# A hybrid layer on one core: tokens also passed transposed, k and v of tile one computed by token, and small VectorE steps woven into other work

## The chip, the core and the metric

The kernel runs on one core of a Trainium2 chip. The metric is the device time of one execution in microseconds (us), as the median over the runs shown. A profile of one execution comes with it: for each engine the instructions with their times, waits and the source lines that issued them. The engines are TensorE (PE in the profile, its weight loads PEld), VectorE (DVE), ScalarE (ACT), GpSimd (POOL) and SyncE (SP, which here only issues DMA transfers).

## What is computed

One decoder layer on 2048 tokens of 1024 channels, in float32. A normed input feeds one projection whose columns are split into nine parts; a short convolution branch and a sliding-window attention branch follow; their projections are merged by gates and added to the input.

```python
h = rms_norm(x, norm_g)                       # x: 1 x 2048 x 1024
u = h @ w_in                                  # conv v, B, C, z | q, k, v, z_a | gates
y_c = b_c * causal_depthwise_conv(c_c * v_c, conv_w) * silu(z_c)
y_a = y_c @ w_conv_out
q = rms_norm(q, q_norm_g); k = rms_norm(k, k_norm_g)     # 16 q heads, 4 k/v heads of 64
o = sliding_window_attention(q, k, v, sinks) * silu(z_a) # window 128, a sink per head
y_b = o @ w_attn_out
g_a, g_b = split(sigmoid(gate_logits + gate_b))
out = x + (g_a * y_a + g_b * y_b) @ w_out
```

`rms_norm` divides each token (each head of a token, for q and k) by the root of its mean square and multiplies by a gain per channel. So `h = x * g * r`, with a root `r` for each token; and since `r` is one number for a token, `h @ w = r * ((x * g) @ w)`.

## The kernel before

**Precision.** Float32 products are made from pairs: each operand is split into a high part (rounded to the matmul's input type, a cast on ScalarE) and a low part (what the cast left out, a subtraction on VectorE), and each product is three matmuls, high x high, high x low, low x high (lines 362 to 371).

**Tiles and units.** Tokens are taken in two tiles of 1024, each in two halves of 512 (`H`), each half in four blocks of 128. Channels come in eight chunks of 128 (`KC`). The activations are kept with channels on partitions and tokens along the free axis, so that a matmul has a 128x128 block of weights as its stationary operand and 512 tokens as the moving one. Most of the work is done in units `sunit` (line 379): a 256-column by 1024-token piece of a projection in seven products instead of eight, in the manner of Strassen. A unit's products run in the order 1, 5, 6, 2, 7, 3, 4, twelve matmuls each. The weights of a unit are prepared by `pieces_of` (264): two loads, high and low parts, and four 128x1024 additions or subtractions (`sums`, 292) for the operands that are sums. The token operands of the seven products are sums and differences of the two halves and of neighbouring chunks; they are kept in `ops`, and made by `form` (545, one split of a chunk held in `raw`) or `direct` (500, a split straight out of PSUM). In tile one, k and v are the exception: `cunit` (409) makes them by channel with the four plain blocks, eight products of 12 matmuls for each, so only operands 1, 2, 8 and 3 are needed for them.

**Order.** The schedule is manual: each engine executes its instructions in the order in which the code issues them. `run` (line 555) drives a unit; each step of twelve matmuls is a tick. After a tick's matmuls it issues the weight loads that have room, the high part of a prepared weight piece (ScalarE), whatever was put down for that tick with `put(n, f)` (551), and then the low part of the weight piece (VectorE). `mids` holds work issued in the middle of a product of `cunit`. So the place of every small step is a number written by hand. SP issues the loads of weights and of attention's operands; POOL issues the stores of q, k and v to DRAM and the token loads of tile two.

**The start** (lines 1107 to 1214). SP loads four token tiles of 128 x 1024 (`x_load`), the first weight half, four more token tiles, and the next weight halves. ScalarE sums the squares (`x_square`); VectorE makes the roots in a chain of some eleven small dependent steps (`x_rsqrt`, `rsqrt` at 191), and the tokens are scaled (`x_scales`). TensorE transposes each chunk of a half with four 128x128 transposes (`x_turn`, 480), and the operands come out of PSUM with the gain applied (`direct`, `x_raw`, `less`). The gains, the convolution taps, the biases and the sinks are loaded as rows by ScalarE's and POOL's queues and transposed on TensorE (`prep_gain`, `prep_cols`). Before all of it TensorE runs 23 and then 14 clearing matmuls on a tile of zeros (`WARM`, `WARM2`, lines 1131 to 1138). Then come k and v of the first half, k and v of the second, and the four q units; the operands of the second half and the sums are put between them.

**After the projection of q.** The conv units, gates and z units follow, with attention steps (`att_load` to `att_out`) put between them, then `ya` and `yb`, the two branch projections (line 970). While `yb` of tile one runs, `next_tile` (1235) prepares tile two: POOL loads the tokens, ScalarE squares them, VectorE makes roots and scales, and `turn_l`/`turn_r` transpose the 64 blocks and make the operands. Tile two then goes the same way, with k and v as units `sunit`. `out` (`fin_o`) ends the kernel.

**q, k and v.** A q result goes through `fin_q` (595): copied from PSUM, split, stored to DRAM by POOL's queue, transposed in groups of four (`turn4`), squared and reduced per head, its roots made at a later tick. `fin_k` (637) transposes k, norms it, transposes it back (`back`) and stores its parts; `fin_v` (682) transposes v and stores it. Attention loads all of it back.

Of the kernel before, what the change touches and what calls it, by code (L numbers as in the profile page):

```python
# [31 lines left out]
WARM = 24  # L32
WARM2 = 14
# [10 lines left out]
def block_kernel(  # L44
# [3 lines left out]
    norm_g: bass.AP,  # L48
    w_in: bass.AP,
    conv_w: bass.AP,  # L50
    q_norm_g: bass.AP,
    k_norm_g: bass.AP,
    sinks: bass.AP,
    w_conv_out: bass.AP,
    w_attn_out: bass.AP,
    gate_b: bass.AP,
# [6 lines left out]
    x2, out2, w_in2 = x[0], out[0], w_in[0]  # L63
# [48 lines left out]

    ident = consts.tile([P, P], F32, name="ident")
# [10 lines left out]
    for h in range(2):  # L124
        nc.vector.tensor_copy(mask_i[HALVES[h]], mask_f[HALVES[h], h, :])
    negc = consts.tile([P, HD], F32, name="negc")
    nc.gpsimd.memset(negc, NEG)
    zero = slot([P, H], F32R, "zero")
    zf = zero.bitcast(F32)
    nc.gpsimd.memset(zf, 0.0)  # L130

    sink_bc = consts.tile([P, NH], F32, name="sink_bc")

    sink_r = consts.tile([P, NKV, 2, 2], F32, name="sink_r")
    nsink_r = consts.tile([P, NKV, 2, 2], F32, name="nsink_r")


    R_B, R_Q = 3 * KC, 5 * KC
    NR = 5 * KC + 2
    rows_g = slot([KC, P], F32, "rows_g")  # L140
    nc.scalar.dma_start(rows_g, norm_g.rearrange("o (c p) -> (o c) p", p=P))
    cols_g = consts.tile([P, KC], F32, name="cols_g")
    rows = slot([NR, P], F32, "rows")

    def load_rows(xt):

        seen = small.tile([P, 1], F32, tag="sx", bufs=4, name="seen")
        nc.gpsimd.tensor_copy(seen, xt[:, 0:1])
        nc.gpsimd.dma_start(sink_bc, sinks.partition_broadcast(P))
        nc.gpsimd.dma_start(rows[0:R_B, :], conv_w.rearrange("t (c p) -> (t c) p", p=P))  # L150
        nc.gpsimd.dma_start(rows[R_B:R_Q, :], gate_b.rearrange("o (c p) -> (o c) p", p=P))
        for i, gsrc in enumerate((q_norm_g, k_norm_g)):
            for j in range(2):
                nc.gpsimd.dma_start(rows[R_Q + i : R_Q + i + 1, j * HD : (j + 1) * HD], gsrc)

    cols = consts.tile([P, NR], F32, name="cols")
# [8 lines left out]
    def prep_gain():  # L165
        pt0 = mbank("ptg")
        nc.tensor.transpose(pt0[:, 0, :KC], rows_g, ident[:KC, :KC])
        nc.vector.tensor_copy(cols_g, pt0[:, 0, :KC])

    def prep_cols():  # L170
        pt0 = mbank("pt0")
        nc.tensor.transpose(pt0[:, 0, :NR], rows, ident[:NR, :NR])
        nc.vector.tensor_copy(cols, pt0[:, 0, :NR])
        nc.vector.tensor_scalar(
            out=gqk, in0=cols[:, R_Q : R_Q + 1], scalar1=cols[:, R_Q + 1 : R_Q + 2],
            scalar2=HD ** -0.5, op0=ALU.mult, op1=ALU.mult)
        nc.vector.tensor_scalar(
            out=hbias, in0=cols[:, R_B:R_Q], scalar1=0.5, scalar2=None, op0=ALU.mult)
        sv = sink_bc.rearrange("p (j c e) -> p j c e", c=2, e=2)
        for e in range(2):  # L180
            for h in range(2):
                nc.vector.tensor_copy(sink_r[HALVES[e], :, h, :], sv[HALVES[e], :, :, e])
        nc.vector.tensor_scalar(out=nsink_r, in0=sink_r, scalar1=-1.0, scalar2=None, op0=ALU.mult)
# [7 lines left out]
    def rsqrt(a, n, name):  # L191
# [3 lines left out]
        nc.vector.tensor_scalar(  # L195
            out=t.bitcast(I32), in0=a.bitcast(I32), scalar1=1, scalar2=None,
            op0=ALU.logical_shift_right)
        nc.vector.tensor_scalar(
            out=r.bitcast(I32), in0=t.bitcast(I32), scalar1=-1, scalar2=RSQRT_MAGIC,
            op0=ALU.mult, op1=ALU.add)  # L200
        for _ in range(3):
            nc.vector.tensor_tensor(out=t, in0=r, in1=r, op=ALU.mult)
            nc.vector.scalar_tensor_tensor(
                out=t, in0=t, scalar=-0.5, in1=a, op0=ALU.mult, op1=ALU.mult)
            nc.vector.scalar_tensor_tensor(
                out=r, in0=t, scalar=1.5, in1=r, op0=ALU.add, op1=ALU.mult)
        return r

    def split(hi, lo, src):
        nc.scalar.copy(hi, src)  # L210
        return nc.vector.tensor_tensor(out=lo, in0=src, in1=hi.bitcast(F32), op=ALU.subtract)  # L211

    def add(o, a, b, eng=None):
        return (eng or nc.vector).tensor_tensor(out=o, in0=a, in1=b, op=ALU.add)  # L214

    def sub(o, a, b, eng=None):
        return (eng or nc.vector).tensor_tensor(out=o, in0=a, in1=b, op=ALU.subtract)

    def mul(o, a, b, eng=None):
        return (eng or nc.vector).tensor_tensor(out=o, in0=a, in1=b, op=ALU.mult)  # L220
# [6 lines left out]
    def load_half(i=None, first=None):  # L227
# [8 lines left out]
        if kind in "SC":  # L236
            raw = rawpool.tile([P, 2, KP, P], F32, tag="raw", name=name)
            if first:
                first(raw)
# [24 lines left out]
    def pieces_of(n):  # L264
# [7 lines left out]
        def two(hi, lo, src):  # L272
            return (lambda: nc.scalar.copy(hi, src),
                    lambda: nc.vector.tensor_tensor(
                        out=lo, in0=src, in1=hi.bitcast(F32), op=ALU.subtract))

        if kind in "SC":
# [11 lines left out]
            if kind == "C":  # L289
                return w, [(2, 1, lambda h=h: pair(h, (h, 0), (h, 1), f"c{h}")) for h in range(2)]  # L290

            def sums():
                ra, rb = raws[2 * n], raws[2 * n + 1]

                def f():
                    sub(ra[:, 0], ra[:, 0], rb[:, 0])
                    add(rb[:, 0], rb[:, 0], rb[:, 1])
                    sub(rb[:, 1], rb[:, 1], ra[:, 0])
                    sub(ra[:, 1], ra[:, 1], rb[:, 1])

                return (lambda: None, f)

            return w, [(2, 0, lambda: pair(0, 1, 2, "a")), (1, 0, single), (0, 0, sums),
                       (2, 1, lambda: pair(1, 5, 6, "s")), (2, 1, lambda: pair(0, 7, 3, "t"))]
# [17 lines left out]
    def piece():  # L322
# [4 lines left out]
        need = [2 * n + i] if plan[n][0] in "TC" else [2 * n, 2 * n + 1][: 1 + min(i, 1)]  # L327
# [32 lines left out]
    mids = {}  # L360
# [18 lines left out]
    def sunit(key, ops, fin):  # L379
# [7 lines left out]
        yield  # L387
        vb = bank(f"V{nm}")
# [7 lines left out]
        product(xb, u, 2, ops, False)  # L396
        fin(0, 0, xb)
        yield
# [10 lines left out]
    def cunit(key, ops, fin, q, hold):  # L409

        if q == 0:
            hold[key] = unit(key)
        u = hold[key]
        for i in range(2):
            ps = bank(f"C{key[0]}_{i}_{q}")
            for p in range(2):
                force(u, (i, p))
                hi, lo = ready[u][i, p]
                for j in range(KP):
                    b = ops[B_AT[p, q]][j]  # L420
                    for n, (w, m) in enumerate(((hi, 0), (hi, 1), (lo, 0))):
                        nc.tensor.matmul(
                            ps, lhsT=w[:, j, :], rhs=b[:, m, :], start=p == 0 and j == 0 and n == 0,
                            stop=p == 1 and j == KP - 1 and n == 2)
                    if j == 1:
                        for f in mids.pop(tick[0], []):
                            f()
                if p == 0:
                    yield
            fin(i, q, ps)  # L430
            live[0] -= 2 * q
            yield

    def into(dst, val):
        if isinstance(val, tuple):
            add(dst, *val)
        else:
            nc.scalar.copy(dst, val)
# [9 lines left out]

    def x_load(t, b, eng):
# [5 lines left out]
    def x_square(xt, junk, ss, i):  # L455

        nc.scalar.activation(out=junk, in_=xt, func=AF.Square, accum_out=ss[:, i : i + 1])

    def x_rsqrt(t, b0, n, ss):
        ms = small.tile([P, n], F32, tag="sm", name=f"ms{t}_{b0}")  # L460
        nc.vector.tensor_scalar(out=ms, in0=ss, scalar1=1.0 / D, scalar2=EPS, op0=ALU.mult, op1=ALU.add)
        return rsqrt(ms, n, f"hr{t}_{b0}")

    def x_scale(xt, r, i, act, cs=slice(0, D)):
        if act:
            nc.scalar.activation(out=xt[:, cs], in_=xt[:, cs], func=AF.Copy, scale=r[:, i : i + 1])
        else:
            nc.vector.tensor_scalar(
                out=xt[:, cs], in0=xt[:, cs], scalar1=r[:, i : i + 1], scalar2=None, op0=ALU.mult)

    def x_scales(xs, q, r):
        for i in range(HB):
            xt = xs[q * HB + i]
            if i < 3:
                x_scale(xt, r, i, i == 2)
            else:
                x_scale(xt, r, i, False, hs(0))
                x_scale(xt, r, i, True, hs(1))

    def x_turn(t, q, c, xs, pt=None):  # L480
        if pt is None:
            pt = mbank(f"pth{t}_{q}_{c}")
        for b in range(HB):
            nc.tensor.transpose(pt[:, b, :], xs[q * HB + b][:, c * P : (c + 1) * P], ident)
# [888 lines left out]
```

## Time and profile before

| what | us |
|---|---|
| median of three runs | 2014.37 (2012.85 to 2015.1) |
| the profiled execution | 2012.82 |
| its span, first to last instruction | 2011.1 |

Where TensorE stands in that span, from the busy time by stretch (PE busy, VectorE busy):

| stretch, us | length | PE | DVE | what runs |
|---|---|---|---|---|
| 0 to 13.59 | 13.59 | 10.96 | 4.82 | loads, squares, roots; clearing matmuls |
| 13.59 to 98.55 | 84.96 | 80.48 | 71.21 | k and v of tile one, the first q unit |
| 98.55 to 162.09 | 63.54 | 63.27 | 50.64 | the three other q units |
| 162.09 to 861.00 | 698.91 | 695.04 | 480.53 | conv, gates, z, attention, ya |
| 861.00 to 948.33 | 87.33 | 87.33 | 60.65 | yb; tile two prepared |
| 948.33 to 2011.10 | 1062.8 | 1055.1 | 715.6 | tile two and out |

The last row is two stretches added. A busy share is read with care: the clearing matmuls of the first 13.59 us are busy time too, and they compute nothing of the result. The granted TensorE clock is 1.00 in all rows, which is the hardware's full rate.

### The profile page before, as it was taken

The numbers are of one execution on the slowest core, as the hardware profiler recorded it, in microseconds if no ns is written. First come the engines' busy times: TensorE is split into PE (matmuls) and PEld (weight loads), VectorE is DVE, ScalarE is ACT, GpSimd is POOL, SyncE is SP. The second block draws the span as 40 slices with busy tenths as digits, with TensorE's granted clock in tenths as the row PEclk, the third lists the DMA queues.
The fourth block names the chain that finished last, engine by engine and source line by source line (L and its number), as shares of the span: only waits on it lengthen the run. The fifth ranks groups of instructions, "written<-read, shape, count | busy, mean of one in ns | idle before, by whom it ended". The sixth has DMA issues, their size and how long they took to land.

```text
span 2011.1 us, 27717 instructions
## 1 busy us (share of the span) xinstructions
PE 1992.2 (99%) x9360; PEld 1656.5 (82%) x9360; DVE 1383.4 (69%) x2361; ACT 934.0 (46%) x1847; POOL 375.3 (19%) x521
## 2 busy tenths in 40 slices
PE   8999999999999999999999999999999999999999
PEld 6788888888888888888888888888888888888887
DVE  6878878787775565358777887887776656356654
ACT  7554454456664343244555454556665334212321
POOL 1462222123330000000263212212322000100000
PEclk9999999999999999999999999999999999999999
DMA  5485444457564535764486434555665434865553
GB/s 170 126 216 129 130 122 131 121 164 203 163 184 159 182 105 173 231 208 155 113 211 173 120 109 134 142 142 176 184 187 185 151 122 147 259 210 168 169 173 110
DMA packets 336317, 324.61 MB, mean 161 GB/s; under 512 B 25788, under 2 KB 256240, under 8 KB 336176
## 3 DMA queue, kind: packets, MB, share of 16 engines
q1 hardware_dynamic: 323136, 284.78, 47.1%
q0 software_dynamic: 13024, 38.06, 7.3%
q8 instruction: 75, 1.23, 0.3%
q14 instruction: 66, 0.54, 0.1%
q10 hardware_dynamic: 16, 0.00, 0.0%
HBM read 226.00 MB, written 96.73 MB: 160 GB/s over the span
## 4 chain that ended last, share of the span: by engine, by line
PE 90%; DVE 4%; ACT 3%; issue 2%; DMA 1%; POOL 0%; SPq 0%; POOLq 0%; ACTq 0%; DVEq 0%
PE Y L368 28%; PE yb L970 9%; PE ya L970 8%; PE Xcv L368 4%; PE Vcv L368 4%; PE Vb L368 2%; PE Xb L368 2%; PE Xza L368 2%; PE Vz L368 2%; PE Vo L368 2%; PE Xz L368 2%; PE Xo L368 2%; PE Vza L368 2%; PE po L840 2%; PE Vq L368 2%; PE Xq L368 2%
## 5 line engine op out<-in xcount | busy, mean ns | idle before, releaser
L823 POOL TENSOR_SCALAR_AFFINE_SELECT xh<-xh 64x512 fp32r<-64x512 f32 x64 | 67.6, 1056 | 654.8 <-DVE xl L815 524.3
L794 ACT ACTIVATE p<-s,st,rq 128x128 f32<-128x128 f32 x256 | 113.3, 453 | 0.5
L214 DVE TENSOR_TENSOR o<-po,o 64x256 f32<-64x256 f32 x128 | 53.7, 419 | 58.6 <-ACT o L851 56.2
L1004 DVE SCALAR_TENSOR_TENSOR tha<-tha,ya 128x512 f32<-128x512 f32 x32 | 22.0, 688 | 92.4 <-PE ya L970 90.7
L851 ACT COPY o<-po 64x256 f32<-64x256 f32 x128 | 47.0, 367 | 82.4 <-DVE o L214 80.9
L815 DVE TENSOR_TENSOR xl<-pt,xh 128x512 fp32r<-128x512 f32 x64 | 44.2, 691 | 56.0 <-ACT yp L814 49.0
L970 PE MATMUL ya<-opa,wya_1h 128*128 128x512 f32 x256 | 79.6, 391 | 0.9 <-ACT opa L210 0.5
L368 PE MATMUL Xcv<-oph,wcv_ah 128*128 128x512 f32 x256 | 79.8, 393 | 0.0
L970 PE MATMUL yb<-opb,wyb_0h 128*128 128x512 f32 x256 | 79.5, 392 | 0.0
L970 PE MATMUL yb<-opb,wyb_1h 128*128 128x512 f32 x256 | 79.5, 392 | 0.0
L970 PE MATMUL ya<-opa,wya_0h 128*128 128x512 f32 x256 | 78.9, 389 | 0.0
L210 ACT CAST opb<-ocr 128x512 fp32r<-128x512 f32 x32 | 19.9, 621 | 112.2 <-DMA ocr<-ocd 107.2
L1024 DVE SCALAR_TENSOR_TENSOR thb<-thb,yb 128x512 f32<-128x512 f32 x32 | 22.0, 686 | 55.2 <-PE yb L970 55.2
L970 PEld LDWEIGHTS ya<-opa,wya_1h 128*128 128x128 f32 x256 | 48.1, 188 | 12.2 <-ACT opa L210 1.3
L698 POOL DMA_DIRECT2D vd<-v x32 | 20.2, 637 | 200.6 <-DVE v L211 197.6
L970 PEld LDWEIGHTS ya<-opa,wya_0h 128*128 128x128 f32 x256 | 48.1, 188 | 10.0
L970 PEld LDWEIGHTS yb<-opb,wyb_1h 128*128 128x128 f32 x256 | 47.6, 188 | 9.6
L970 PEld LDWEIGHTS yb<-opb,wyb_0h 128*128 128x128 f32 x256 | 47.6, 188 | 9.6
L368 PEld LDWEIGHTS Xcv<-oph,wcv_ah 128*128 128x128 f32 x256 | 47.0, 188 | 9.0
L823 POOL TENSOR_SCALAR_AFFINE_SELECT yp<-xl 64x512 fp32r<-64x512 f32 x64 | 53.6, 838 | 3.1
L889 DVE SCALAR_TENSOR_TENSOR y<-u,cols,y 128x512 f32<-128x512 f32 x64 | 49.1, 767 | 6.2 <-ACT y L882 5.0
L813 ACT CAST xh<-pt 128x512 fp32r<-128x512 f32 x64 | 37.4, 585 | 33.4 <-PE pt L810 32.2
(586 smaller groups left out, 6281.5 us busy)
## 6 DMA issues: line engine op xcount, KB each, us to landing
wcv_raw<-in_w_in SPq DMA_DIRECT2D x64, 256.0 KB, 3.7
q<-q2d SPq DMA_DIRECT2D x64, 256.0 KB, 4.1
v<-vd SPq DMA_DIRECT2D x128, 128.0 KB, 3.3
gd<-th SPq DMA_DIRECT2D x64, 256.0 KB, 2.3
wq_raw<-in_w_in SPq DMA_DIRECT2D x32, 256.0 KB, 4.5
q2d<-q_h POOLq DMA_DIRECT2D x64, 128.0 KB, 3.8
q2d<-q_l POOLq DMA_DIRECT2D x64, 128.0 KB, 4.1
kq<-q2d SPq DMA_DIRECT2D x128, 64.0 KB, 4.0
```

The costliest lines, as they stand in the source:

```text
L214: return (eng or nc.vector).tensor_tensor(out=o, in0=a, in1=b, op=ALU.add)
L368: nc.tensor.matmul(ps, lhsT=w[:, j, :], rhs=b[:, m, :], start=start and j == 0 and i == 0, stop=j == KP - 1 and i == 2, skip_group_check=n ...
L794: nc.scalar.activation(out=p[:, i, :], in_=sg[:, i, HD : 3 * HD], func=AF.Exp, bias=st[:, 1, i : i + 1], scale=rv[:, i // 2, i % 2 : i % 2 ...
L813: nc.scalar.copy(xh, pt)
L815: nc.vector.tensor_tensor(out=xl, in0=pt, in1=xh.bitcast(F32), op=ALU.subtract)
L823: nc.gpsimd.affine_select(out=d4, in_=s4, pattern=[[0, 2 * G], [-sg, HD]], compare_op=ALU.is_gt if prev else ALU.is_ge, fill=0.0, base=0, ...
L840: nc.tensor.matmul(po[:, cs], lhsT=v2[:, kind, :], rhs=xx.rearrange("p g q -> p (g q)")[:, cs], start=n == 0, stop=n == 2)
L851: nc.scalar.copy(ov, pov[oth, :, :, e, :])
L889: nc.vector.scalar_tensor_tensor(out=y, in0=u[:, h * H + i : h * H + i + H], scalar=tap(i, k), in1=y, op0=ALU.mult, op1=ALU.add)
L970: nc.tensor.matmul(ps, lhsT=w[:, j, cs], rhs=o[:, m, :], start=n == 0 and i == 0, stop=n == KC - 1 and i == 2)
L1004: nc.vector.scalar_tensor_tensor(out=m, in0=m, scalar=1.0, in1=ps, op0=ALU.add, op1=ALU.mult)
L1024: nc.vector.scalar_tensor_tensor(out=m, in0=m, scalar=1.0, in1=ps, op0=ALU.add, op1=ALU.mult)
```

## The change

The inputs now also hold `xt`, the tokens transposed (1024 channels by 2048 tokens), and `consts`, one array with taps, biases, q and k gains, gains and sinks already laid out by partition; both are laid out by the host without arithmetic (`_layout`).

*Tile one, loads.* SP alternates chunk halves of `xt` (128x512, 256 KB) with w pieces of a new kind "R": 128 rows by 512 columns, k and v side by side. The natural token tiles are still loaded, behind them, but only for the sums of squares.

```diff
+    FIRST_X = {(0, 0): (1,), (0, 1): (2, 3), (1, 0): (4,), (1, 1): (5,), (2, 0): (6,), (2, 1): (7,)}
...
+    xt_load(0, 0)
+    for n in range(3):
+        load_half(n)
+    xs[0] = x_load(0, 0, nc.sync)
+    load_half(3)
+    for b in range(1, HB):
         xs[b] = x_load(0, b, nc.sync)
+    for c in range(KC):
+        xt_load(c, 1)
     for b in range(HB, NB):
         xs[b] = x_load(0, b, nc.sync)
...
-    for _ in range(WARM - 1):
-        clear()
-    prep_gain()
-    for _ in range(WARM2):
-        clear()
+    for _ in range(WARM):
+        nc.tensor.matmul(Y, lhsT=zero[:, :P], rhs=zero, start=True, stop=True)
```

`WARM` is 10 (24 and 14 before), and the zeros are written by VectorE instead of POOL. The eight loads of constants as rows and the two transposes of them go, with the copies of sinks into place.

*Tile one, k and v by token, from unscaled tokens.* `plain_op` splits a chunk with the gain but without the root. In `kv_by_token` the tokens are stationary (128 of them) and 512 columns of k and v move, so a result has tokens on partitions: eight banks, the same 192 matmuls. The root of a token is then a number for a partition, and is applied when the result leaves PSUM, in the class `KV`, which takes the place of `cunit`, `fin_k` and `fin_v` in tile one.

```diff
+    def plain_op(c, q):
+        o = new_op("p", B_AT[c % 2, q], c // 2, plain_ops)
+        h = raw[c, q]
+        nc.scalar.activation(out=o[:, 0], in_=h, func=AF.Copy, scale=gain(c))
+        vec.scalar_tensor_tensor(
+            out=o[:, 1], in0=h, scalar=gain(c), in1=o[:, 0].bitcast(F32),
+            op0=ALU.mult, op1=ALU.subtract)
...
+                for k, (m, w) in enumerate(((0, hi), (0, lo), (1, hi))):
+                    nc.tensor.matmul(
+                        ps, lhsT=x[:, m, i * P : (i + 1) * P], rhs=w[:, c % 2],
+                        start=c == 0 and k == 0, stop=c == KC - 1 and k == 2)
...
+            for b in (2 * n, 2 * n + 1):
+                v = slot([P, NKV, 2, HD], F32R, f"v0_{b}")
+                src = self.banks[b][:, UC:].rearrange("p (j d) -> p j d", d=HD)
+                r = rtok[:, b : b + 1]
+                nc.scalar.activation(out=v[:, :, 0], in_=src, func=AF.Copy, scale=r)
+                vec.scalar_tensor_tensor(
+                    out=v[:, :, 1], in0=src, scalar=r, in1=v[:, :, 0].bitcast(F32),
+                    op0=ALU.mult, op1=ALU.subtract)
```

The first eight ticks make the four blocks of the first half, chunk by chunk as the loads land (two score banks and two others); two groups of four ticks make the second half. k is still transposed back (`back`), v no longer is transposed.

*Turned roots.* For q and all that follows, the tokens must be scaled where tokens lie along the free axis. `x_roots` broadcasts each column of 128 roots and transposes it, so every partition gets the roots as a row; `x_norm` multiplies a chunk half by gain and row in one step. It replaces scaling and transposing the tokens in both tiles; the sums for the operands, which `less` made out of PSUM, become plain subtractions (`first_sum`, `second_sum`, `third`, `t4`).

```diff
+    def x_roots(t, q, rs):
+        pt = mbank(f"ptr{t}_{q}")
         for b in range(HB):
+            nc.tensor.transpose(pt[:, b, :], rs[:, b : b + 1].to_broadcast([P, P]), ident)
+        rb = slot([P, H], F32, f"rb{t}_{q}")
+        nc.scalar.copy(rb, pt.rearrange("p b q -> p (b q)"))
+        return rb
...
+    def x_norm(h, c, rb):
+        vec.scalar_tensor_tensor(
+            out=h, in0=h, scalar=gain(c), in1=rb, op0=ALU.mult, op1=ALU.mult)
...
+    put(3, lambda: roots(0))
+    put(6, lambda: turned(0))
...
+    put(6, lambda: norm_l(0, 2, st))
...
+    put(8, lambda: form(0, 1, 1, st))
```

The places of these steps over ticks 1 to 21 are again written by hand (some 80 `put` lines, of which four are shown).

*Woven steps.* All VectorE operations of the kernel now go through `vec`, which issues one waiting step of a chain behind each operation; the chains are the roots (`rsqrt`) and three of the four weight sums. Five more are issued at each tick's end (`WOVEN`), and whoever needs a chain's result issues what is left of it.

```diff
+        def some(self, n):
+            for _ in range(n):
+                self.one()
+        def __getattr__(self, name):
+            f = getattr(nc.vector, name)
+            def g(*args, **kw):
+                r = f(*args, **kw)
+                self.one()
+                return r
+            return g
```

*Tile two.* `next_tile` loads `xt` of tile two chunk by chunk (`raw_load`, 16 loads on POOL's queue), beside the natural tokens for the squares; two groups of four transposes make the root rows, and `norm_l`, `norm_r` and the sums take the place of `turn_l` and `turn_r`.

*Smaller.* The split of q of the first unit is put three ticks later (`QWAIT`); the casts of a mask go from VectorE to POOL. `sunit` gets an order in which product 2 comes second; with `Q_TWO = 0` it isn't used.

By count, TensorE loses 144 transposes (160 go, 16 come) and 28 clearing matmuls, VectorE gains 42 two-tensor steps of 512 and loses 8 scalings and 3 steps of 1024, ScalarE loses 23 steps of 512 and 6 of 1024 and gains 12 copies, POOL gains 16 loads and loses 7, SP gains 24 loads of 256 KB.

More of the change, by code (lines that the diff above doesn't have):

```diff
@@ L110, in hs @@
         return slice(q * H, (q + 1) * H)
+    cols = consts.tile([P, NC], F32, name="cols")
+    nc.scalar.dma_start(cols, consts_in)
+    zero = slot([P, H], F32R, "zero")
+    zf = zero.bitcast(F32)
+    nc.vector.memset(zf, 0.0)
+    seen = small.tile([P, 1], F32, tag="sx", bufs=4, name="seen")
+    nc.scalar.activation(out=seen, in_=zf[:, 0:1], func=AF.Square)
     ident = consts.tile([P, P], F32, name="ident")
@@ L124, in block_kernel @@
     for h in range(2):
-        nc.vector.tensor_copy(mask_i[HALVES[h]], mask_f[HALVES[h], h, :])
+        nc.gpsimd.tensor_copy(mask_i[HALVES[h]], mask_f[HALVES[h], h, :])
     negc = consts.tile([P, HD], F32, name="negc")
     nc.gpsimd.memset(negc, NEG)
[L128 to L134, printed above, removed]
-    nsink_r = consts.tile([P, NKV, 2, 2], F32, name="nsink_r")
[L138 to L156, printed above, removed]
+    sink_r = cols[:, C_S:NC].rearrange("p (j h c) -> p j h c", h=2, c=2)
+    nsink_r = consts.tile([P, NKV, 2, 2], F32, name="nsink_r")
     gqk = consts.tile([P, 1], F32, name="gqk")
@@ L387, in sunit @@
         yield
+        if two:
+            product(xb, u, 2, ops, False)
+            fin(0, 0, xb)
+            yield
         vb = bank(f"V{nm}")
@@ L395, in sunit @@
         yield
-        product(xb, u, 2, ops, False)
-        fin(0, 0, xb)
-        yield
+        if not two:
+            product(xb, u, 2, ops, False)
+            fin(0, 0, xb)
+            yield
         product(Y, u, 7, ops, False)
```

632 lines of the change are left out of this document (366 added, 266 removed).

## The prediction

> **What bounds the kernel now.** I read the page first: busy shares and the chain of work that ended last.
>
> ```profile
> PE 1992.2 (99%) x9360; PEld 1656.5 (82%) x9360; DVE 1383.4 (69%) x2361; ACT 934.0 (46%) x1847; POOL 375.3 (19%) x521
> ...
> PE 90%; DVE 4%; ACT 3%; issue 2%; DMA 1%; POOL 0%; SPq 0%; POOLq 0%; ACTq 0%; DVEq 0%
> ```
>
> TensorE holds nine tenths of the chain, so a microsecond counts only if it is TensorE work or a hole in TensorE. Next, busy time by stretch.
>
> ```profile
> 0.00:10.00 10.00, 7.37 (x24) 5.67 (x24) 1.87 (x2) 5.88 (x9) 4.40 (x17) 1.00 0.74 260
> 20.00:30.00 10.00, 8.36 (x39) 5.66 (x38) 8.65 (x12) 8.78 (x15) 0.00 (x0) 1.00 0.71 187
> 80.00:90.00 10.00, 10.00 (x52) 8.26 (x51) 8.98 (x15) 5.47 (x10) 4.86 (x8) 1.00 0.49 132
> 920.00:930.00 10.00, 10.00 (x52) 8.24 (x51) 7.04 (x12) 4.23 (x7) 0.00 (x0) 1.00 0.71 205
> ```
>
> Columns are the length, then busy time of PE, its weight loads, DVE, ACT and POOL, the granted clock, DMA share, GB/s. TensorE has holes only before some 65 us; VectorE stands near 0.9 from 20 to 100 us, so a start in which TensorE is quicker meets VectorE at once. At 920 TensorE is full and VectorE at 0.70. Then the timeline: two landmarks, and what transposes cost.
>
> ```profile
> 98.55 0.71 PE L368 MATMUL Xq<-oph,wq_ah 128*128 128x512 f32 x2
> 162.09 0.71 PE L368 MATMUL Xcv<-oph,wcv_ah 128*128 128x512 f32 x2
> 903.49 0.39 PE L970 MATMUL yb<-opb,wyb_0l 128*128 128x512 f32 x1
> 903.72 0.60 PE L484 MATMUL pth<-ident,x 128*128 128x128 f32 x4
> 904.07 0.71 PE L970 MATMUL yb<-opb,wyb_1h 128*128 128x512 f32 x2
> ```
>
> Four transposes put off the next matmul from 903.72 to 904.07: 0.35 us. A 128x512 matmul follows the last after 0.227 us (903.49 to 903.72). The second q unit begins at 98.55, the first conv unit at 162.09; from 98.55 on, both kernels run the same units. Last, VectorE's pitch, and the first loads as ScalarE meets them.
>
> ```profile
> 5.74 1.06 ACT L457 ACTIVATE wk_raw<-x 128x1024 f32<-128x1024 f32 x1 [0.20 <-DMA x<-in_x]
> 7.05 1.06 ACT L457 ACTIVATE xsq<-x 128x1024 f32<-128x1024 f32 x1 [0.16 <-DMA x<-in_x]
> ...
> 24.30 0.74 DVE L504 SCALAR_TENSOR_TENSOR oph<-pth,cols_g,oph 128x512 fp32r<-128x512 f32 x1
> 24.95 0.74 DVE L1178 TENSOR_SCALAR h<-pth_x,cols_g 128x512 f32<-128x512 f32 x1
> ...
> 62.31 1.22 DVE L274 TENSOR_TENSOR wq_al<-wq_raw,wq_ah 128x1024 fp32r<-128x1024 f32 x1
> 63.44 0.69 DVE L211 TENSOR_TENSOR oph<-h,oph 128x512 fp32r<-128x512 f32 x1
> 64.40 0.17 DVE L177 TENSOR_SCALAR hbias<-cols 128x16 f32<-128x16 f32 x1
> 64.48 0.49 DVE L182 COPY sink_r<-sink_bc 64x8 f32<-64x8 f32 x4
> ...
> 109.17 0.18 DVE L195 TENSOR_SCALAR q_t<-q_ms 128x32 int32<-128x32 int32 x1
> 109.39 0.18 DVE L198 TENSOR_SCALAR q_r<-q_t 128x32 int32<-128x32 int32 x1
> ```
>
> Start to start, a 128x512 step takes 0.61 with two tensors, 0.66 with a scalar column, a 128x1024 one 1.13. A small step that waits for the one before takes 0.20 to 0.22; one that waits for nothing lets the next start 0.08 later. That difference is all that weaving can save. Each x tile (512 KB) lands 1.31 us after the one before.
>
> **The change, part by part.** *Start, loads.* Landing at 512 KB per 1.32 us, with the flow beginning 1.3 us ahead of the first square at 4.40: the chunks of transposed x alternate with w chunks of 256 KB, the last w half is number 18 of 24, at 3.1 + 9 x 1.32 = 15.0, x3 at 18.9. All issues are SP's (0.45 us each, four in 1.81) and keep ahead. TensorE: ten clears at 0.43 apart end near 5.6, as the first w and x parts are split; 12 matmuls a chunk are 2.7 us, while ScalarE (two casts, 1.2) and VectorE (two subtractions, 1.3) make a chunk in half of that. So the 27 clears dropped cost nothing while the clock comes up, as it does after some 4 us of clears now.
>
> *Start, the roots.* ScalarE splits the last w at 16.1, then squares four x tiles at 1.18 apart (24.06, 25.24, 26.43 in its rows): 20.9. VectorE then begins the roots and is the later engine from there on. From there to the last operand of the first q unit (opening part 4, second pair) its queue holds 24 scalar-column steps of 512 (16.0 us), 55 two-tensor steps or reductions of 512 (33.6), 3 chained sums at 0.72 (2.2), 4 of 1024 (4.5), 4 of 256 (0.42 long, 0.35 apart: 1.4), 17 small chained (3.4) and 21 woven (1.7): 62.8, with 0.8 of waits for ScalarE's v parts 84.5. TensorE alone needs 276 matmuls (62.6) and four groups of transposes (1.4) from 5.6: it would be there at 69.6, so it waits for VectorE three times on the way: for the roots of the first half (needed at 21.9, there at 25.7), for the low part of wq_0 (needed about 54, there at 56.9) and for its sums' low part (68.2). With half a product left, the second q unit starts at 86.0 instead of 98.55: 12.5 earlier. Behind it five more groups of transposes than before are still due (two of k, three of q, 17 against 12): 1.8 lost. The conv units start 10.7 earlier, at 151.4.
>
> The scaling by turned roots is not in the trace (both operands in SBUF). Its bounds: 0.66, as the steps from PSUM above, and 0.80, the 767 ns of y<-u plus the wait of a held step; I take 0.667, nearest by form, so 16 such steps give -0.1 to +2.1. The one load of the constants is ScalarE's: between 4 us (beside the first x) and 9 (the 7.9 us to landing of rows<-in_conv_w); I take the first, since nothing is queued ahead of it, and the second would push ScalarE's 16 splits and all behind them by 3. Transposes with a broadcast operand: 0.09 to 0.33 each (a transpose alone lasts 0.27), 16 of them, 0 to +3.
>
> *Clock.* Granted clock is 1.00 in all early rows; after the last matmul (2007.2) the stretch 2010.0 to 2011.1 shows 0.64, so it halves 3.1 us later. My wait for the roots is 3.8 us. [...]
>
> *Tile two.* Its 64 transposes stand at 878 to 929, in a full TensorE: four groups of eight at 0.80 and eight of four at 0.35, 6.0 us. Two groups of four replace them: 5.3 gained. VectorE gets 16 scalings and 12 subtractions for 12 scalar-column subtractions and 4 scalings: about +7.5 us over 70 us in which it is 0.36 to 0.99 busy; most fall before 930, where it fits. If that cover fails, the first k unit (948) waits for them, at most 5. Sixteen loads more on POOL's queue (0.53 each) fall where POOL is idle for 134 us; behind them stand only one another.
>
> *The rest.* From the first conv unit on, the order on all queues is as before but for the root chains of k and q and the weight sums, woven; q results are due dozens of steps later, so nothing waits, and 0. The three-step delay of q's first parts: 0, as attention loads them 20 steps later.
>
> Sum: 10.7 + 5.3 = 16.0. The profiled execution took 2012.8 (span 2011.1, 1.7 around it): 1996.8. The median of the runs, 2014.4, is 1.6 above it: 1998.4. I say **1998**.
>
> **Rivals.** (1) *TensorE sets the start*, VectorE keeping up: second q unit at 69.6, 16.4 more: 1982. For: PE holds 90% of the chain. Against: VectorE's 62.8 us of queue. 8%. (2) *Tile two gives nothing*, its first k unit waiting for VectorE: 2003 to 2004. For: VectorE is 0.99 and 0.94 busy from 930 to 950. Against: the steps added there are few. 9%. (3) *The opening flow is slow.* 6.3 MB (24 pieces of 256 KB) must land before the roots, over some 15.8 us, so at 398 GB/s; every microsecond later shifts VectorE's whole queue. At 250 GB/s x3 lands 9.4 later: 2008. At 170 it lands at 40, 21 later: **2019, slower than before**; it is slower than the measurement can excuse (2018.4) from a delay of 20, some 175 GB/s. For: before, the stretches 8 to 10, 10 to 12 and 12 to 14 us moved 246, 213 and 214 GB/s. Against: there 512-byte pieces of w and POOL's small loads mix in; x alone ran at 412 from 4 to 6 us. 10% for 2004 to 2010, 5% for the slower end. (4) *The clock stays half* through the waits of the start: 276 matmuls at 0.43 are 118 us, q unit two at about 125: 2040. For: the wait of 3.8. Against: waits under it follow, and TensorE is dense between. 1%.
>
> **Numbers.** Forecast 67%, by itself 1993 to 2003 (the bounds above; runs spread 2.3). To it come rival 2 (9%) and the milder flow cases up to 2006 (6 of the 10%), so **1986 to 2006** leaves out most of rival 1 (7), the later flow cases (4), the slow end (5) and rival 4 (1): 17%. What 0.2% (4.0 us) cannot tell from no change is 2010.4 to 2018.4. Faster: the forecast and rivals 1 and 2, 84%, and the flow cases that end before 2010.4, 7: 0.91. Same: 0.04, out of the flow cases between; slower: 0.05, the slow end beyond 2018.4 and rival 4.
>
> **What would show it.** The conv units at 151 us; VectorE near full from 21 to 90; a hole of 3 to 4 us in front of the first turned roots; the second q unit at 86; TensorE full from 860 to 960 with two groups of transposes. Wrong if VectorE idles in the start, if the first product of k and v starts after 8 us, or if the first k unit of tile two waits.

## The result and the profile after

The changed kernel takes 2002.64 us (median of four executions, 2001.58 to 2004.0), the kernel before 2014.73 in the same comparison: a ratio of 0.9942, with a 95% interval of 0.9925 to 0.9959. That is 12.1 us gained where 16.4 were forecast. The profiled execution took 2004.0, the longest of the four, with a span of 2002.3, so 8.8 of span against the profile of before. (In a later repeat one execution ran at a mean granted clock of 0.81 and took 2266.64 us; neither its time nor its trace is read.)

The page first, with the two lines that were shown of before.

```profile
PE 1974.9 (99%) x9186; PEld 1641.4 (82%) x9186; DVE 1396.3 (70%) x2402; ACT 920.6 (46%) x1835; POOL 378.1 (19%) x530
...
PE 89%; DVE 4%; ACT 2%; DMA 2%; issue 2%; SPq 0%; POOL 0%; DVEq 0%; ACTq 0%; POOLq 0%
```

Nothing in these says where the gain went. The busy time by stretch does (length, then PE, PEld, DVE, ACT and POOL busy, granted clock, DMA share, GB/s).

```profile
20.00:30.00 10.00, 6.57 (x26) 5.18 (x25) 7.81 (x23) 8.88 (x16) 0.00 (x0) 0.78 1.04 397
30.00:40.00 10.00, 10.00 (x41) 8.13 (x40) 8.87 (x26) 8.69 (x19) 2.08 (x4) 0.88 0.90 216
...
60.00:70.00 10.00, 3.79 (x16) 2.40 (x14) 9.90 (x17) 4.06 (x6) 0.00 (x0) 0.82 0.01 2
70.00:80.00 10.00, 9.25 (x28) 7.40 (x29) 9.48 (x15) 4.81 (x8) 2.36 (x4) 0.66 0.65 157
80.00:90.00 10.00, 10.00 (x48) 8.28 (x47) 9.93 (x16) 6.82 (x13) 2.28 (x4) 1.00 0.37 92
```

VectorE is full from 60 to 90 us, as forecast. New is the column of the granted clock: before, it was 1.00 in every row of the start. A mean of 0.66 over 10 us means 6.8 us at half rate (from 66.48 to 76.72 the mean is 0.50, from 77 to 78 it is 1.00); from 70 to 80 TensorE is busy 9.25 of 10 us and gets 28 matmuls done, where the next row has 48. The view of waits names the holes ahead of it.

```profile
PE Vq L405 <- ACT wq_sh L300: 4.4, 1, 4.4
PE ptr L504 <- DVE rtok L498: 3.4, 1, 3.4
...
PE Vq L405 <- DVE wq_sl L203: 2.6, 1, 2.6
...
PE Xq L405 <- DVE wq_al L203: 1.3, 1, 1.3
PE ptr L504 <- DVE rt L498: 1.2, 1, 1.2
```

The columns are the total, the number and the longest of the waits. `ptr<-rtok` is the wait for the first roots; the two waits of Vq come one behind the other, with two matmuls of product 5 of the first q unit between them, and make a hole of 7 us that ends at 70.75. The last line is in tile two. The landmarks on TensorE's timeline, and VectorE's last operand of the first q unit (the line at 37.14 is read in the section on the prediction):

```profile
90.00 0.62 PE L405 MATMUL Xq<-oph,wq_ah 128*128 128x512 f32 x2
156.37 0.71 PE L405 MATMUL Xcv<-oph,wcv_ah 128*128 128x512 f32 x2
937.65 0.61 PE L405 MATMUL Xk<-oph,wk_ah 128*128 128x512 f32 x2
```

```profile
21.73 0.17 DVE L217 TENSOR_SCALAR ms<-ss 128x4 f32<-128x4 f32 x1 [3.04 <-ACT x L494]
...
37.14 0.48 DVE L203 SCALAR_TENSOR_TENSOR v<-kv,rtok,v 128x256 fp32r<-128x256 f32 x1 [0.95 <-ACT v L625]
...
58.29 1.22 DVE L203 TENSOR_TENSOR wq_al<-wq_raw,wq_ah 128x1024 fp32r<-128x1024 f32 x1
...
69.48 1.22 DVE L203 TENSOR_TENSOR wq_sl<-wq_raw,wq_sh 128x1024 fp32r<-128x1024 f32 x1
...
86.13 1.29 DVE L203 TENSOR_TENSOR oph<-t,oph 128x512 fp32r<-128x512 f32 x2
```

| landmark, us | before | forecast | after |
|---|---|---|---|
| roots of the first half begin | | 20.9 | 21.73 |
| first turned roots on TensorE | | 25.7 | 26.88 |
| low part of wq_0 done | | 56.9 | 59.5 |
| low part of the weight sums done | | 68.2 | 70.7 |
| second q unit | 98.55 | 86.0 | 90.00 |
| first conv unit | 162.09 | 151.4 | 156.37 |
| from there to tile two's k | 786.2 | 780.9 | 781.3 |
| from there to the `out` units | 906.4 | 906.4 | 908.2 |

The start gave 5.7 us instead of 10.7, tile two 5.0 instead of 5.3, and 1.8 were lost late in tile two, where none was forecast.

### The profile page after: what moved, and what is told of

It is laid out like the page before. It is cut to its first block, busy times and chain, and to the rows that moved or that the text cites. A ratio compares the mean times of both kernels' runs of the same rounds, so it can differ in the third digit from the quotient of the medians.

```text
span 2002.3 us, 27428 instructions
## 1 busy us (share of the span) xinstructions
PE 1974.9 (99%) x9186; PEld 1641.4 (82%) x9186; DVE 1396.3 (70%) x2402; ACT 920.6 (46%) x1835; POOL 378.1 (19%) x530
## 4 chain that ended last, share of the span: by engine, by line
PE 89%; DVE 4%; ACT 2%; DMA 2%; issue 2%; SPq 0%; POOL 0%; DVEq 0%; ACTq 0%; POOLq 0%
PE Y L405 29%; PE ya L1058 8%; PE yb L1058 8%; PE Xcv L405 4%; PE Vcv L405 4%; PE Vb L405 2%; PE Xb L405 2%; PE Xza L405 2%; PE Vz L405 2%; PE Vo L405 2%; PE Xo L405 2%; PE Xz L405 2%; PE Vza L405 2%; PE Vq L405 2%; PE po L928 2%; PE Xq L405 2%
## 5 line engine op out<-in xcount | busy, mean ns | idle before, releaser
L203 DVE SCALAR_TENSOR_TENSOR thb<-thb,yb 128x512 f32<-128x512 f32 x32 | 21.9, 685 | 43.7 <-PE yb L1058 41.5
L1146 POOL DMA_DIRECT2D wo<-in_w_out x16 | 8.7, 541 | 226.8 <-DVE opb L203 209.7
```

The costliest lines, as they stand in the source:

```text
L203: r = f(*args, **kw)
L1146: nc.gpsimd.dma_start(h, w_o[c * P : (c + 1) * P, hs(q)])
```

## The experiments

Unless said otherwise, each is the changed kernel with one edit. Two more numbers are compared than the time: where the second q unit and the first conv unit begin. Kernels with the same start as the changed one (e4 and e8 below) show how these spread between executions: 88.35, 88.91 and 90.00 for the second q unit, 154.70, 155.33 and 156.37 for the conv units. A difference of 1.5 us in one trace is therefore no verdict. Part of it lies ahead of the first roots, which VectorE begins at 21.72 to 22.87 in the traces with the new loads; where it matters, the start is counted from there.

**Eight VectorE steps left out (e6).** Leaves out the subtractions `first_sum` and `second_sum` of tile one.

```diff
-    put(13, lambda: first_sum(0, st))
...
-    put(17, lambda: second_sum(3, st))
```

> Leaves out the eight subtractions that make operands 5 and 6 of tile one's q out of the scaled chunks (the unscaled difference is simply not taken), 8 x 0.61 = 4.9 us of VectorE ahead of the first q unit's last operand. Theory (VectorE's queue): the second q unit 4 to 5 us earlier, at 85 to 86. Rival (TensorE with its clock): at most 1.5 earlier.

Measured: the second q unit at 83.92, 4.4 to 6.1 earlier than with the steps, and the conv units at 149.96. The one execution took 1997.07. VectorE's queue sets the start. (Part of the 4.4 to 6.1 is clock: this trace has one half-rate stretch in the start, of 6.83 us, where the three unedited starts have two. Against e11 below, whose clock is full and whose second q unit begins at 87.69, it is still 3.8 earlier.)

**TensorE kept busy in its holes (e1).** Twelve clearing matmuls ahead of the first turned roots, thirty dummies ahead of product 5, into a bank that the next product overwrites.

```diff
+        if (t, q) == (0, 0):
+            for _ in range(12):
+                nc.tensor.matmul(
+                    pt.rearrange("p b q -> p (b q)"), lhsT=zero[:, :P], rhs=zero, start=True, stop=True)
...
+        if key == ("q", 0, 0):
+            for _ in range(30):
+                nc.tensor.matmul(
+                    vb, lhsT=ready[u][1][0][:, 0, :], rhs=ops[1][0][:, 0, :], start=True, stop=True)
         product(vb, u, 5, ops, True)
```

> 12 clearing matmuls ahead of the first turned roots and 30 dummy matmuls (into the bank that the next product overwrites) ahead of product 5 of the first q unit, where TensorE waits 3.4 and 4.4 + 2.6 us and then runs 6.8 and 10.2 us at half clock. Theory (VectorE's queue paces the start, the half clock costs only what sticks out behind VectorE's last operand at 87.4, and some of VectorE's waits for k and v): the second q unit begins at 88 to 89.2 instead of 90.0, the time falls by 1 to 2 us. Rival (the half clock is what the start lacks, 2.4 + 3.1 us of TensorE work lost): the second q unit at 84.5 to 86, 4 to 5.5 us faster.

Measured: 1999.18 us (1998.71 to 1999.84), 3.5 less than the changed kernel. The second q unit began at 88.49, within what the theory said, but that is also within the spread of the unedited start. Counted from the first roots, which came late in this execution (22.87), it is clear of the unedited starts: 65.62 us, against 68.27, 67.05 and 66.46 in the changed kernel, e4 and e8. One half-rate stretch of 3.41 us was left, from 59.88. The time fell by more than the start shows; this is taken up with the repeat below.

**Product 2 second (e5).** `Q_TWO = 1` uses the order of `sunit` that the change brought and left unused, so that TensorE has 2.7 us of work in the hole.

```diff
-Q_TWO = 0
+Q_TWO = 1
...
-    put(18, lambda: form(0, 2, 3, st))
+    put(17, lambda: form(0, 2, 3, st))
```

> The first q unit makes product 2 as its second, so TensorE has 2.7 us of work in the hole of 4.4 us ahead of product 5. All else stays in place. Theory (VectorE's queue): the last operand comes when it came, only the half clock behind the hole goes: second q unit at 88 to 89.2, 1 to 2 us faster. Rival (TensorE's hole and half clock): 4 us and more, at 86 or earlier.

Neither came: 2007.7 us, 5.1 slower, the second q unit at 95.30. Its ScalarE timeline shows why.

```profile
57.34 0.60 ACT L230 CAST oph<-xt 128x512 fp32r<-128x512 f32 x1
65.11 1.04 ACT L300 CAST wq_sh<-wq_raw 128x1024 fp32r<-128x1024 f32 x1 [7.17 <-DVE wq_raw L203]
66.06 0.61 ACT L230 CAST oph<-xt 128x512 fp32r<-128x512 f32 x1
66.58 0.58 ACT L423 COPY Y<-Xq 128x512 f32<-128x512 f32 x1
```

Product 2 adds to the bank of product 1, so it must wait until ScalarE has copied that bank to Y. The copy stands in order behind the cast of the weight sums, which itself waits 7.17 us for VectorE. The hole is the same, and product 2 lies behind it.

**k's roots later (e2, e9).** Ticks 24 to 31, then 28 to 41, instead of 12 to 28.

```diff
-    KV_AT = {"p": (9, 8, 14, 21), "v": (10, 8, 23, 40), "r": (12, 22), "b": (17, 21, 27, 28)}
+    KV_AT = {"p": (9, 8, 14, 21), "v": (10, 8, 23, 40), "r": (24, 28), "b": (26, 27, 30, 31)}
```

e9 has `"r": (28, 36), "b": (31, 33, 39, 41)`.

> The roots, scaling and transposing back of k of tile one at ticks 24 to 31 instead of 12 to 28. Theory (VectorE's queue): the chain of twelve small steps (1.6 us), two scalings (1.2) and one low part of k (0.6) leave the queue ahead of the first q unit's last operand, so that the second q unit begins 2 to 3.4 us earlier, at 86.6 to 88, and 2 to 3 us are gained in all. Rival (TensorE with its half clock paces): under 0.7. A second rival: the steps come back in the second and third q unit, where VectorE is 97% busy, and the conv units begin no earlier than 156.4.

> As the run with k later, but at ticks 28 and 36 (transposing back at 31 to 41), spread over the third q unit and the first conv units; k's first reader is due at tick 60. Theory (VectorE's queue paces the start, and k later lost only because its two chains met the reductions that TensorE's transposes of q wait for): the second q unit at 85 to 87 again, and with the two chains eight ticks apart most of it stays, conv units at 152.5 to 154.5, 2 to 4 us faster than the changed kernel. Rival (VectorE's queue is full to the conv units, so that steps moved out of the first q unit are paid later): conv units at 156 or after, no gain.

In both the second q unit came as early as hoped, at 85.65 and 86.20: steps taken out of VectorE's queue are gained there. But the conv units began at 160.44 and 162.99, and the times are 2006.68 and 2009.48. The waits of e2 show the place:

```profile
PE pbk L649 <- DVE qss L203: 4.6, 1, 4.6
```

k's transposing back waits for a bank that a reduction of q's squares (`qss`) must free, and that reduction stands on VectorE behind k's chain, its scalings and the weight sums. A half-rate stretch of 3.41 us follows this wait (from 115.67). VectorE is not full ahead of it (7.14 of 10 us from 100 to 110 in e2) but is while TensorE waits (9.30 from 110 to 120), so it looks as if the order costs, and not the load alone; no run puts the reduction ahead of the other steps. Spreading them in e9 moved the collision to q's own chain (3.1 and 1.8 us of `ptq` waits), without removing it. The outcomes that e2's second rival and e9's rival named are what came.

**No weaving (e3).** `chain` issues all its steps at once, and k's second chain one tick later.

```diff
         def chain(self, *steps):
+            for f in steps:
+                f()
+            return lambda: None
...
-"r": (12, 22)
+"r": (12, 23)
```

> Every chain issues its steps at once instead of one behind each other VectorE step (the second k chain of tile one one tick later). Theory (VectorE's queue paces the start): some 14 steps ahead of the first q unit's last operand lose their cover, 14 x 0.12 = 1.7 us, against which the first roots come 2.4 us earlier and TensorE's first hole (3.4) nearly closes; the second q unit at 90 to 91.5, the rest unchanged, 2002.6 to 2004.5. Rival (the weaving is what brought the gain): back by 4 us or more, 2006 and above. Second rival (weaving the first roots under four other steps costs more than it saves): faster than with it, under 2002.

The rival came: 2007.91 us (2006.23 to 2009.04), 5.3 slower; the second q unit at 91.69, the conv units at 160.06. The first of TensorE's waits closed as expected (`ptr` waits 1.0 instead of 3.4), but others opened:

```profile
PE Xq L408 <- DVE wq_al L206: 4.8, 1, 4.8
PE Vq L408 <- DVE wq_sl L206: 4.5, 2, 3.1
PE kvb L462 <- DVE v L206: 3.5, 1, 3.5
```

In the last line TensorE, 4.8 us ahead of the changed kernel there, meets v's low part, which frees a bank for the last blocks of k and v and is done 1.5 later than there (45.2 instead of 43.7): a VectorE that is later gives nothing for a TensorE that is earlier. At the second q unit it is 1.7 to 3.3 late, against 1.7 expected for 14 uncovered steps; from there to the conv units it takes 68.4 us instead of 66.4, where the chains of k and q stand undivided ahead of the reductions that free TensorE's banks (one such wait shows, 0.9 us of pbk for qss). So weaving is worth 4 to 5 us at the conv units (5.3 in the time), and the forecast's "all that weaving can save" had only the steps' own time in the start.

**Eight sums on GpSimd (e7).** `third` and `t4` of tile one.

```diff
-        sub(o, raw[2 * j + 1, 0], raw[2 * j, 0])
+        sub(o, raw[2 * j + 1, 0], raw[2 * j, 0], None if to is None else nc.gpsimd)
...
-        sub(raw[c - 1, 1], raw[c, 1], raw[c - 1, 1])
+        sub(raw[c - 1, 1], raw[c, 1], raw[c - 1, 1], eng)
...
```

> The eight subtractions of tile one's start that are due last (for operands 7 and 4 of q) on GpSimd instead of VectorE. Theory (VectorE's queue): 8 x 0.61 = 4.9 us less in it, so the second q unit at 84 to 86 as where eight steps were left out (83.9), 4 to 6 us faster, if a GpSimd subtraction takes under 2.5 us. Rival: GpSimd's steps are slow or slow VectorE's, so that operand 7 or 4 is late or VectorE's pitch rises: no gain or a loss.

The rival came: 2005.79 us, the second q unit at 93.83. Its timelines of GpSimd and of VectorE, the same stretch:

```profile
77.90 1.31 POOL L237 TENSOR_TENSOR xt<-xt,xt 128x512 f32<-128x512 f32 x1
79.16 3.77 POOL L237 TENSOR_TENSOR t<-xt,xt 128x512 f32<-128x512 f32 x3
```

```profile
75.74 1.21 DVE L203 TENSOR_TENSOR wq_tl<-wq_raw,wq_th 128x1024 fp32r<-128x1024 f32 x1
78.06 5.42 DVE L203 TENSOR_TENSOR oph<-xt,oph 128x512 fp32r<-128x512 f32 x1 [1.12 <-ACT oph L230]
83.41 0.68 DVE L203 TENSOR_TENSOR Vq<-s5q,Y 128x512 f32<-128x512 f32 x1
```

A GpSimd subtraction takes 1.3 to 1.8 us, under the 2.5 that were allowed. But VectorE's step of 0.69 takes 5.42 us while four of them run, and ends 0.55 behind the last of them, some of its own length. With four other steps that grew by 1.0 to 1.1 each, VectorE lost some 9 us for the 4.9 taken off it. Why VectorE's steps grow is not shown.

**Tile two as before (e8).** The 64 transposes, scaled tokens and sums out of PSUM put back in `next_tile`.

```diff
-            put(n0 + 15 + j, lambda j=j: norm_r(t, 2 * j, st))
-            put(n0 + 16 + j, lambda j=j: first_sum(j, st))
+            put(n0 + 16 + j, lambda j=j: turn_r(t, 2 * j, st))
...
```

> Tile two prepared as before the change (64 transposes, scaled tokens, sums out of PSUM), all else as changed. Theory: the 5.0 us that the traces show between the conv units of tile one and the first k unit of tile two come from these transposes, so the time is 5 us longer, 2006.5 to 2008. Rival: half of it or more comes from elsewhere: under 2005.

Measured: 2007.07 us (2006.21 to 2009.14), and 787.05 from the conv units to tile two's k against 781.28. As expected: tile two's part is 5.0 us between the kernels and 5.8 in this run.

**Tile two's second roots a tick later (e4).**

```diff
-        for q, n in enumerate((8, 15)):
+        for q, n in enumerate((8, 16)):
...
-            put(n0 + 15 + j, lambda j=j: norm_r(t, 2 * j, st))
+            put(n0 + 16 + j, lambda j=j: norm_r(t, 2 * j, st))
```

> In tile two the second turning of roots and what needs it (the scalings of the even chunks' second halves) one tick later, where TensorE now waits 1.15 us for the last root. Theory: the wait goes and nothing else is late, since k's first operands of the second half are due 40 us later: the first k unit of tile two 1.1 earlier against the conv units, 6.1 to 6.2 gained there instead of 5.0. Rival: the wait moves on to an operand: no change.

The wait of 1.15 went, but from yb to k of tile two it took 88.79 instead of 89.41, 0.6 less where 1.1 were expected; and e12 below has no such wait without the edit (88.03). The time, 2000.49 (1999.29 to 2001.17), differs from the changed kernel's by 2.2, most of it elsewhere. What the edit is worth stays open.

**The repeat, one group of dummies, and both improvements (e13, e12, e11).** e13 is the changed kernel unaltered, e12 is e1 with the thirty dummies alone (the diff is against e1), e11 is e1 with e4's edit, all three on one chip.

```diff
-            for _ in range(12):
+            for _ in range(0):
```

> The changed kernel unaltered, beside the next two: 2001.5 to 2004; half-clock stretches of 6.8 to 13.7 us in all between 20 and 90 us, their length differing between executions in steps of 3.41 us, and the conv units at 154.7 to 156.4 accordingly.

> Only the 30 dummy matmuls ahead of product 5 of the first q unit, none ahead of the first turned roots. Theory (the second hole's half clock sticks out, the first one's is absorbed in the wait for wq_0's low part): conv units at 154.7 to 155.3, 1 to 2 us faster than the changed kernel beside it, within 0.7 of both dummies together. Rival (the first hole's half clock delays k and v and so VectorE): under 0.7 faster.

> Both groups of dummy matmuls and the later turning of roots in tile two. Theory: 2 to 3.5 us from the clock and 0.6 from tile two, 1998 to 1999.5, faster than the changed kernel and than each alone. Rival: the two gains were spread of the runs, under 1.5 in all.

Measured: e13 2001.92 to 2004.47 in four executions; its trace isn't read, so what was expected of its clock is answered by the traces of e4 and e8 instead. e12 1999.89 (1999.26 to 2000.82), e11 1999.37 (1998.92 to 2000.37; ratio to before 0.9927, interval 0.9915 to 0.9940). In e11 the clock is full through the whole start:

```profile
60.00:70.00 10.00, 9.12 (x43) 7.23 (x42) 9.90 (x16) 4.08 (x6) 0.00 (x0) 1.00 0.00 0
70.00:80.00 10.00, 9.64 (x42) 7.64 (x43) 10.00 (x17) 6.04 (x11) 2.37 (x4) 1.00 0.75 182
```

and its second q unit begins at 87.69, VectorE being as full as ever. e12 has the first half-rate stretch (6.83 us from 26.4) and begins it at 89.15, no earlier than the unedited starts; its conv units, at 155.57, miss the 154.7 to 155.3 of its theory. The first hole's half rate does reach VectorE, as e12's rival said (the section on the prediction shows where). In time, e12 gained 2.5 on e13 beside it, more than either named.

The three kernels with dummies took 1998.71 to 2000.82 in 14 executions, the changed kernel 2001.58 to 2004.47 in eight, so the gain of some 3 us is sure; and their mean granted clock was 0.998 to 1.000, the changed kernel's 0.995 to 0.997. e11 is not told apart from e1, so beside the dummies e4's edit adds nothing that shows. What the dummies gain is only in part where they stand: at the second q unit e11 is 0.7 to 2.3 ahead of the three unedited starts. From the conv units to the last instruction the profiled execution of the changed kernel took 1845.9 us, e1, e11 and e12 1843.2 to 1843.8: in these three neither the half-rate stretch in attention nor the wait of 1.15 us in tile two came (both are taken up below). Whether the dummies keep them away is open.

## Why the prediction was near, and where it fell short

**What bounds the kernel, and the start's mechanism: right.** VectorE sets the pace from the roots on (e6, and e2's and e9's second q unit). The queue itself was sized well: from 21.73 to the end of its last needed operand at 87.4 are 65.7 us; its waits in that stretch (0.19, 0.95, 0.54, 0.52 and 0.52) are 2.7, which leaves 63.0 against the 62.8 of the forecast. The price of scaling by turned roots, seven steps in 4.72, is 0.66 (29.31 to 33.95), as taken.

**Loads and squares: 0.8 late.** ScalarE waits 1.39 us for the last w pieces, so that the squares begin at 17.43 instead of some 16.2; they follow one another after 1.04 instead of 1.18, and the roots begin at 21.73 instead of 20.9. The flow was 383 GB/s from 3 to 19 us, near the 398 of the forecast; the slow flow (rival 3) did not come.

**VectorE's waits: mis-sized.** 0.8 were forecast for v's parts, 2.7 came. With the clock kept full (e11) they are 1.1 (0.19, 0.36 and 0.54), so the other 1.6 are the clock's. e11's second q unit still begins 1.7 later than forecast: 1.1 by late roots (22.00), 0.3 by these waits, and 0.3 because it begins 1.8 behind VectorE's last operand where the forecast had 1.5.

**The clock: the step that failed.** The forecast's sum has nothing for half rate behind the first wait (3.8 us). That was the author's estimate; no run shows that such a wait is free, and what the runs showed for the start is 0.8 to 2.6 us (the table below). Its own numbers had a second and longer hole, from the end of the first product (begun at 56.9) to 68.2, and it put no clock against that. In the profiled execution TensorE ran at half rate (a granted clock of 0.50) for 6.83 us from 25.52 and for 10.24 us from 66.48, of which 6.0 lie behind the second hole. What this cost shows when the start is counted from the first step of the roots, for which the forecast had 65.1:

| kernel | half-rate stretches in the start, us | roots to second q unit, us |
|---|---|---|
| changed | 6.83 and 10.24 | 68.27 |
| e4 | 6.83 and 6.83 | 67.05 |
| e8 | 3.41 and 10.24 | 66.46 |
| e12 | 6.83 | 67.09 |
| e1 | 3.41 | 65.62 |
| e11 | none | 65.69 |

So the half rate cost 0.8 to 2.6 us (e1's stretch, which begins at 59.88 in the first product, ahead of the dummies, nothing), and most of it came by way of VectorE, which the forecast had as the pacing engine. Behind a first stretch of 6.83 us, TensorE finishes k and v later, ScalarE copies them later, and VectorE waits for v's part (the line at 37.14 above) and then 0.52 for the second row of roots. In e11 the second wait is absent and the first is short:

```profile
36.83 0.48 DVE L203 SCALAR_TENSOR_TENSOR v<-kv,rtok,v 128x256 fp32r<-128x256 f32 x1 [0.36 <-ACT v L633]
...
84.85 3.01 PE L405 MATMUL Y<-oph,wq_d 128*128 128x512 f32 x12 [0.41 <-DVE q_t L203]
```

Behind a second stretch of 10.24 us, VectorE waits 0.52 for a cast that stands on ScalarE behind the late copy of product 5, and TensorE itself comes late to product 4 (`Y<-oph,wq_d`): 1.06 us behind the step of VectorE that lets it begin (`q_t`, done at 86.22), where e11 shows 0.15. In the profiled execution these four are 0.6, 0.5, 0.5 and 0.9, together 2.5 of the 2.6. Of the 4.0 us missing at 90.00, the clock is thus 2.6, the late roots 0.8, and the rest 0.6.

**From the second q unit to the conv units** 65.4 were forecast and 66.4 came, in the changed kernel as in e4, e8 and e11: five more groups of transposes, as counted, and 1.0 more, which the forecast had at nothing. One wait of it shows, 0.48 of `ptq` for `q_t`.

**Tile two: right.** 5.3 forecast, 5.0 measured, 5.8 with the part undone. One of the two groups of transposes waited 1.15 us for its roots, in this execution though not in all; the added VectorE steps (9.8 of 10 us busy from 900 to 940) made no operand late. Rival 2 did not come.

**"The rest: 0" was off by 1.8** in the profiled execution, where a half-rate stretch of 3.41 us begins at 1380.6 behind a hole in attention. The hole is older than the change: the same 2.06 us from one matmul to the next stand in every trace, the one of before included. The stretch follows it in five of the thirteen traces read and not in the others, so it is a cost by chance. The kernel before seems to have such stretches too: of its executions beside the experiments, 34 had a mean clock of 1.000 and took 2012.58 to 2014.19, and ten had 0.999, which one stretch of 3.41 us would give, and took 2014.07 to 2016.07. Whether the dummies make it rarer is open: in none of the three traces with them did it come.

**Weaving** was priced as 0.12 us a step in the start and nothing after. It is worth 4 to 5 us at the conv units (e3). That didn't move the sum, since the steps were counted as woven.

TensorE setting the pace (rival 1) was refuted by e6; of the clock's rival (4) a part came, for stretches rather than throughout.

That 2002.64 still lies below the 2003 that the forecast gave itself is luck in part: that room was meant for the turned scaling (up to 2.1), the broadcast transposes (up to 3) and a later load of the constants (3). The first two cost what was taken (0.66 a step, and 0.36 us for four transposes, 43.56 to 43.92); the clock, which had no room of its own, used what they left.

## What to carry to other kernels

Where one engine's queue paces another, a wait has two prices: the wait itself, and the half clock that can follow the hole in TensorE (here behind 2.06 us in five of thirteen traces, and behind 3.4 to 3.9 us ahead of the first turned roots in eight of the nine that left that hole open). The half clock can come back to the pacing engine, as results that it waits for (here 1.6 us of VectorE's 2.7 us of waits in the start). Go through the forecast's own timeline for every such hole, not only for the one that the change is about. Idle TensorE time ahead of dense work can be filled with dummy matmuls into a bank that is overwritten next: 30 to 42 of them took some 3 us off here. Taking steps out of a full in-order queue is worth only what remains after the place where they are put back (e2 and e9 began the second q unit 4.4 and 3.8 us earlier and took 4.0 and 6.8 longer in all): look there for short steps that others wait for. Before another engine is given the work, ask what its steps do to those that stay (in e7, some 9 us lost for 4.9 taken off).

## What the runs showed of the hardware

The stretches at half rate (a granted clock of 0.50) in the thirteen traces that are read here are 3.41, 6.83 or 10.24 us long (leaving out the one after the last matmul, which the end cuts off): one, two or three times 3.41, and the same start got 13.7 us of them in two executions and 17.1 in a third. The same hole of 2.06 us is followed by a stretch in five of these traces and not in the other eight; what decides is not shown here.

While four GpSimd subtractions of 128x512 followed one another in e7 (77.90 to 82.93), one VectorE subtraction of the same size, begun at 78.06, took 5.42 us instead of 0.69 and ended 0.55 behind the last of them; four other VectorE steps that ran beside GpSimd subtractions took 1.0 to 1.1 longer each. What holds them up is not shown.
